# Two attention mixers of an encoder trunk: TensorE's order fixed product by product, scalings moved to ScalarE, and the per-layer input products moved into the mixers' ends

## The chip, the cores and the metric

The kernel runs on one core of one Trainium2 chip. The metric is the device time of one execution in microseconds (us), the median of several runs. The engines are named as the profile names them: PE is TensorE's matrix product, PEld its weight load, DVE is VectorE, ACT is ScalarE, POOL is GpSimd, SP is the queue that issues most transfers (DMAs).

## The reference

A trunk of two layers over 512 positions with a width of 1024, all in float32. Cut to what matters:

```python
for i in range(DEPTH):                                   # DEPTH = 2
    h = h + 0.5 * swiglu(rmsnorm(h), ffn1...)            # inner width 2816
    hn = rmsnorm(h, norm_mix[i])
    if i % 2 == 0:
        h = h + ab_mixer(hn, w_in_ab, sink_a, w_out_ab, pos)
    else:
        h = h + c_mixer(hn, w_in_c, rpb_c, w_out_c)
    h = h + 0.5 * swiglu(rmsnorm(h), ffn2...)
    gate = sigmoid(rmsnorm(h, norm_ple[i]) @ w_ple_gate[i])
    h = h + gate * (p[i] @ w_ple_proj[i])                # p[i]: 512 x 256, an input
return rmsnorm(h, norm_final)
```

`ab_mixer` projects `hn` to queries, keys and values of two kinds of attention. Kind A has 12 query heads and 4 key heads; each block of 128 queries sees its own block of keys and the neighbours, and each head has a sink logit in its softmax. Kind B has 4 slots, each with three groups of keys at strides 1, 4 and 16; the outputs of the groups are merged by weights that come from the maxima and sums of their softmaxes. `c_mixer` is attention of 16 heads over an 8 x 16 neighbourhood of a grid of width 64, with a bias from a table. Each mixer ends with a product by `w_out`. The product `p[i] @ w_ple_proj[i]` depends on inputs alone.

## The kernel before

All activations lie transposed: 8 chunks of 128 channels by 512 positions. To keep float32's accuracy each operand of a large product is split in a high part (rounded to PE's reduced float32, written by ACT) and a low part (the rest, a subtraction on DVE or POOL). One such product (`mm3`) is three matmuls: high by high, high by low, low by high (L142 to L144 of the kernel before, L322 to L324 for the values). A weight unit of 128 x 1024 (512 KB) is fetched by SP as `wr` and split into `wh` (ACT) and `wl` (DVE) at L121 and L122.

The stages in the profile, in us from the span's start: the first feed-forward part to 381, mixer ab from 381 to about 662, the second feed-forward part, the per-layer input stage (`ple`) to about 1100, then the same for layer 1 with mixer c from about 1450 to 1668 and `ple` from about 2063 to 2108, and the tail.

A mixer has two kinds of work for PE. The *fill* is the projections (24 matmuls of 512 columns each for a query or key unit, values by groups of 256 columns), which need only weights and `xg`, the scaled input. The *steps* are attention itself: for each head the scores (L428, L598), a masked maximum on DVE (L429, L602), exponentials on ACT (L568, L608), the scaling by the reciprocal of the sum on DVE (L572, 48 instructions), transposes on PE (L349) into a PSUM bank named `tr`, the split of these by ACT (L121, high) and DVE (L122, low), and the products with the values (L359, L360) into a bank named `ob`. For kind B, `merge` (L611) works out weights by small copies and products on DVE and scales the 32 blocks of exponentials on DVE (L638); `pv_r` transposes those of the strided groups (L647) and multiplies (L653).

PSUM has three banks for products (`mm`), two for scores (`sc`), two for transposes (`tr`) and one for `ob`. A bank is written again only when what it held has been read.

`weave` (L503) calls steps and fills whole, one after the other, in a proportion of weights. The instructions that come of it are put in an order on each engine by the framework's scheduler, by readiness and priority; so PE's order in the program is already mixed instruction by instruction. Once built, every engine runs its own list in order.

Of the kernel before, what the change touches and what calls it, by code (L numbers as in the profile page):

```python
# [15 lines left out]
P = 128  # L16
# [15 lines left out]
PART = .8  # L32
WARM = 12
RPB_W = 48


class Trunk:
# [3 lines left out]
    def __init__(self, ctx, tc, io):  # L41
# [6 lines left out]
        self.ap_ = pool("act", 59)  # L48
        self.tp = pool("tmp", 8)
# [10 lines left out]
        self.open = {}  # L60

# [27 lines left out]

    def setup(self):  # L90
# [5 lines left out]
        self.identb = self.cp.tile([P, P], BF16, name="identb")  # L96
        nc.vector.tensor_copy(self.identb, self.ident)
# [7 lines left out]
        idle = self.cp.tile([P, T], BF16, name="idle")  # L105
# [33 lines left out]
    def mm3(self, out, stat, mov, start, stop):  # L139

        mm = self.nc.tensor.matmul
        mm(out, stat[0], mov[0], start=start, stop=False)  # L142
        mm(out, stat[0], mov[1], start=False, stop=False)  # L143
        mm(out, stat[1], mov[0], start=False, stop=stop)  # L144
# [37 lines left out]
    def stat(self, tag, cols):  # L182
# [3 lines left out]
        for i, x in enumerate(cols):  # L186
            nc.tensor.matmul(ps[:, i:i + 1], self.acc[:, x], self.ones[:, 0:1], start=True, stop=True)
# [13 lines left out]
    def spread(self, rcol):  # L201

        n = rcol.shape[-1]
        rp = self.tbank()[:, :n * P]
        for b in range(n):
            self.nc.tensor.transpose(rp[:, b * P:(b + 1) * P], rcol[:, b:b + 1].broadcast_to([P, P]), self.ident)
        return rp
# [46 lines left out]

    def project(self, src):

        u = self.unit(src, lo_eng=self.lo_eng())
        p = self.bank()
        self.mm_unit(p, u, self.xg, True, True)
        return p  # L260

# [46 lines left out]
    def project_v(self, src, view, rcol, parts=True):  # L308
# [5 lines left out]
        for q in range(2):  # L314
            u = self.unit(src[:, q * UNIT:(q + 1) * UNIT], lo_eng=self.lo_eng())
            for kk in range(4):
                k = 4 * q + kk
                h, l = (x[:, kk * 256:(kk + 1) * 256] for x in u)
                for b in range(NB):
                    xh, xl = (view(x, b) for x in self.xg[k])  # L320
                    first, last = k == 0 and b % 2 == 0, k == KC - 1 and b % 2 == 1
                    nc.tensor.matmul(ps[b], xh, h, start=first, stop=False, skip_group_check=True)  # L322
                    nc.tensor.matmul(ps[b], xh, l, start=False, stop=False, skip_group_check=True)  # L323
                    nc.tensor.matmul(ps[b], xl, h, start=False, stop=last, skip_group_check=True)  # L324
# [18 lines left out]
    def transposed(self, blocks):  # L343
# [4 lines left out]
        for i, b in enumerate(blocks):  # L348
            nc.tensor.transpose(t[:, i * P:(i + 1) * P], b, self.ident)  # L349
        hi, lo = self.tmp(F32R), self.tmp(F32R)  # L350
# [4 lines left out]
    def pv(self, out, v, p, start, stop):  # L355


        mm = self.nc.tensor.matmul
# [3 lines left out]
    def windows_pv(self, o, es, vcol):  # L362

        for x in range(NB):
            qb = range(*self.window(x))
            blocks = []
            for b in qb:
                off = (x - self.window(b)[0]) * P
                blocks.append(es[b][:, off:off + P])
            hi, lo = self.transposed(blocks)  # L370
            self.pv(o[:, qb[0] * P:(qb[-1] + 1) * P], vcol(x), (hi, lo), x == 0, x == NB - 1)

    def out_part(self, w, m, mix, cs):
# [4 lines left out]
        for c in cs:  # L378
            ww = (u[0][:, c * P:(c + 1) * P], u[1][:, c * P:(c + 1) * P])
            self.mm3(p, ww, mix[c], c == 0, c == KC - 1)  # L380
        return p

    def out_proj(self, w, mix, done, k_next):
# [3 lines left out]
        for m in range(KC):  # L387
            p = self.out_part(w, m, mix, range(done if m < OPEN else 0, KC))
            del self.open[m]
            nc.vector.tensor_tensor(self.h[m], p, self.h[m], op=ALU.add)  # L390
            self.norm_chunk(m)

# [25 lines left out]
    def scores(self, q, k, hf, b, m):  # L418
# [6 lines left out]
        e = self.act()[:, :n]  # L425
        qq, kk = slice(b * P, (b + 1) * P), slice(lo * P, hi * P)
        for i in range(2):
            nc.tensor.matmul(s[:, :n], q[hf][:, qq], k[i][hf][:, kk], start=i == 0, stop=i == 1)  # L428
        nc.vector.tensor_tensor_reduce(e, s[:, :n], mask[:, off:off + n], op0=ALU.add, op1=ALU.max, scale=0.125,  # L429
                                       scalar=-3e38, accum_out=st)  # L430
        return e
# [5 lines left out]
    def ab(self, k_next):  # L437
# [20 lines left out]
        def proj(key, i, kind):  # L458
            return key, 1, lambda: t.__setitem__(key, self.rope(self.project(w[i]), kind))

        def proj_a(gp):
            def k_step():
                k, low = self.rope(self.project(w[12 + 4 * gp]), "n"), self.lows()
                t["ak", gp] = (self.stack_k(k, low), low)

            def q_step(j):
                t["aq", gp, j] = self.stack_q(self.rope(self.project(w[13 + 4 * gp + j]), "n"))

            return [(("ak", gp), 1, k_step)] + [(("aq", gp, j), 1, lambda j=j: q_step(j)) for j in range(3)]

        def proj_b(sp):
            def q_step():
                t["bq", sp, 0] = self.stack_q(self.rope(self.project(w[6 * sp]), "b"))

            def k_step():
                k, low = self.rope(self.project(w[6 * sp + 1]), "n"), self.lows()
                t["bk", sp, 0] = (self.stack_k(k, low), low)

            steps = [(("bk", sp, 0), 1, k_step), (("bq", sp, 0), 1, q_step)]
            for g in (1, 2):  # L480
                steps.append(proj(("bq", sp, g), 6 * sp + 2 * g, "r"))
                steps.append(proj(("bk", sp, g), 6 * sp + 2 * g + 1, "r"))
            return steps

        def proj_v(key, i):
            if i < 2:
                f = lambda: v.__setitem__(key, self.project_v(io["v_ab"][i], nat, self.rcol))
            else:
                f = lambda: v.__setitem__(key, self.residues(
                    self.project_v(io["v_ab"][i], nat, self.rcol, parts=False)))  # L490
            return [(key, 2.4, f)]

        a0, a1 = proj_a(0), proj_a(1)
        fill = (a0[:2] + proj_v("va", 0) + a0[2:] + a1 + proj_b(0) + proj_v("vb", 1) + proj_v(("vr", 0), 2)
                + proj_b(1) + proj_v(("vr", 1), 3))
        steps = (self.a_steps(0, t, v, m_a, sink, mix) + self.a_steps(1, t, v, m_a, sink, mix)
                 + self.b_steps(0, t, v, m_b0, m_br, mix) + self.b_steps(1, t, v, m_b0, m_br, mix))
        fill += [(("o", m), PART, lambda m=m: self.out_part(io["o_ab"], m, mix, range(6))) for m in range(OPEN)]
        self.weave(steps, fill, after={("o", 0): 26})
        self.out_proj(io["o_ab"], mix, 6, k_next)  # L500

    @staticmethod
    def weave(steps, fill, lead=1, after=()):  # L503


        by, after = {}, dict(after)
        for i, (needs, _, _) in enumerate(steps):
            for k in needs:
                by.setdefault(k, i)
        end = len(steps) + lead  # L510
        for i in range(len(fill) - 1, 0, -1):
            name, prev = fill[i][0], fill[i - 1][0]
            by[prev] = min(by.get(prev, end), by.get(name, end))
        total, work = sum(f[1] for f in fill), sum(s[1] for s in steps)
        n, done, past = 0, 0, 0
        for i, (_, weight, f) in enumerate(steps):
            while n < len(fill) and after.get(fill[n][0], 0) <= i and (
                    by.get(fill[n][0], end) <= i + lead or (done + fill[n][1]) * work <= past * total):
                done += fill[n][1]
                fill[n][2]()  # L520
                n += 1
            f()
            past += weight
        for _, _, f in fill[n:]:
            f()
# [6 lines left out]
    def a_steps(self, gp, t, v, m_a, sink, mix):  # L532
# [529 lines left out]
```

## Time and profile before

| what | value |
|---|---|
| median of 3 runs | 2126.14 us (2123.86 to 2126.70) |
| the profiled execution | 2126.64 us, of which the span 2124.8 us |
| mean granted clock of PE | 0.995 |
| busy PE, DVE, ACT, POOL | 98%, 53%, 37%, 17% of the span |
| mixer ab, 381 to 675 us: busy PE, DVE, ACT | 275.2, 238.1, 154.4 of 294 us |
| mixer c, 1480 to 1668 us: busy PE, DVE, ACT | 183.3, 139.3, 113.7 of 188 us |

A busy matmul is recorded from its start to a modelled end, and successive matmuls overlap. A row of a matmul of 512 columns says some 390 ns, while in a stretch without a wait one starts every 226 ns. So an idle time of PE is shorter in the record than the time that is lost. The number to compare is the stretch less the number of matmuls times their pace.

### The profile page before, as it was taken

Reading aid. Unit: us, or ns where it says so; the run is one execution under the profiler, and the core shown is the slowest. Engines: PE = TensorE matmul, PEld = TensorE weight load, DVE = VectorE, ACT = ScalarE, POOL = GpSimd, SP = SyncE. Lnnn points to the kernel's source line nnn. Section 1 sums busy time; section 2 is a strip of 40 time slices with the busy share of each in tenths; the row PEclk is TensorE's granted clock in tenths of the full one; section 3 lists DMA queues with packets and bytes.
Section 4 is the critical chain, followed back from the end, with each engine's and each line's share of the span. In section 5 each row is a group of like instructions: output and inputs, shape, how many; then the busy total and the mean of one; then the engine's idle time right before and its main releaser. Section 6 shows DMA issues by size and latency. Waiting matters only on the chain.

```text
span 2124.8 us, 25520 instructions
## 1 busy us (share of the span) xinstructions
PE 2085.4 (98%) x9950; PEld 1734.6 (82%) x9950; DVE 1132.3 (53%) x1793; ACT 783.8 (37%) x1255; POOL 352.3 (17%) x248
## 2 busy tenths in 40 slices
PE   8999999999999999999999999999999999999998
PEld 6888888777787888888888888888888888888886
DVE  6554432699786444543354555333778744553334
ACT  4332222465544333222343233223656533232232
POOL 3111101233211111101111111013222210110111
PEclk9999999999999999999999999999999999999999
DMA  5333333221223233333333322334333223323331
GB/s 171 98 99 99 95 96 98 85 75 56 65 68 92 90 99 99 99 90 96 105 97 99 99 93 93 95 97 124 105 105 102 82 90 99 99 91 96 94 107 60
DMA packets 75385, 202.02 MB, mean 95 GB/s; under 512 B 16896, under 2 KB 24576, under 8 KB 75264
## 3 DMA queue, kind: packets, MB, share of 16 engines
q1 hardware_dynamic: 74976, 200.29, 30.8%
q8 instruction: 78, 1.28, 0.3%
q14 instruction: 43, 0.35, 0.1%
q10 hardware_dynamic: 288, 0.10, 0.0%
HBM read 191.97 MB, written 2.59 MB: 92 GB/s over the span
## 4 chain that ended last, share of the span: by engine, by line
PE 89%; DVE 5%; ACT 2%; issue 1%; POOL 1%; DMA 0%; SPq 0%; DVEq 0%; POOLq 0%; ACTq 0%
PE mm L143 15%; PE mm L144 15%; PE mm L142 15%; PE sc L142 12%; PE sc L143 12%; PE sc L144 12%; PE mm L322 1%; PE mm L323 1%; PE mm L324 1%; PE tr L349 1%; PE ob L359 1%; PE ob L360 1%; PE sc L428 1%; ACT wh L121 1%; DVE act L572 1%
## 5 line engine op out<-in xcount | busy, mean ns | idle before, releaser
L121 ACT ACTIVATE wh<-wr 128x1024 fp32r<-128x1024 f32 (+1 forms) x360 | 374.6, 1042 | 995.0 <-issue 431.1
L122 DVE TENSOR_TENSOR wl<-wr,wh 128x1024 fp32r<-128x1024 f32 (+1 forms) x343 | 510.2, 1488 | 314.1 <-ACT wh L121 313.1
L143 PE MATMUL mm<-act,wh 128*128 128x512 f32 (+1 forms) x1560 | 609.7, 391 | 3.0 <-DVE act L169 2.1
L142 PE MATMUL mm<-act,wh 128*128 128x512 f32 (+1 forms) x1560 | 609.1, 391 | 1.0 <-ACT wh L121 0.6
L144 PE MATMUL mm<-act,wl 128*128 128x512 f32 (+1 forms) x1560 | 608.3, 390 | 0.5 <-DVE wl L122 0.5
L144 PE MATMUL sc<-act,wl 128*128 128x512 f32 (+1 forms) x1138 | 442.5, 389 | 0.8 <-DVE wl L122 0.8
L142 PE MATMUL sc<-act,wh 128*128 128x512 f32 (+1 forms) x1138 | 442.9, 389 | 0.0
L143 PE MATMUL sc<-act,wh 128*128 128x512 f32 (+1 forms) x1138 | 442.5, 389 | 0.0
L143 PEld LDWEIGHTS mm<-act,wh 128*128 128x128 f32 x1560 | 293.4, 188 | 64.4 <-DVE act L169 5.3
L142 PEld LDWEIGHTS mm<-act,wh 128*128 128x128 f32 x1560 | 293.3, 188 | 60.0 <-ACT act L121 1.5
L144 PEld LDWEIGHTS mm<-act,wl 128*128 128x128 f32 x1560 | 293.2, 188 | 58.4 <-DVE wl L122 1.0
L239 POOL TENSOR_TENSOR tmp<-tmp,tmp 128x512 f32<-128x512 f32 x88 | 115.2, 1309 | 818.5 <-DVE tmp L238 783.7
L144 PEld LDWEIGHTS sc<-act,wl 128*128 128x128 f32 x1138 | 213.7, 188 | 45.1 <-DVE wl L122 1.2
L143 PEld LDWEIGHTS sc<-act,wh 128*128 128x128 f32 x1138 | 213.7, 188 | 44.1
L142 PEld LDWEIGHTS sc<-act,wh 128*128 128x128 f32 x1138 | 213.6, 188 | 43.8
L238 DVE TENSOR_TENSOR tmp<-sc,R 128x512 f32<-128x512 f32 x88 | 60.8, 691 | 276.8 <-PE sc L144 276.8
L180 POOL TENSOR_TENSOR ssq<-ssq,tmp 128x512 f32<-128x512 f32 x55 | 90.2, 1639 | 552.6 <-ACT tmp L175 525.7
L236 DVE TENSOR_TENSOR tmp<-mm,R 128x512 f32<-128x512 f32 x88 | 60.8, 691 | 130.4 <-PE mm L144 127.9
L121 ACT ACTIVATE act<-tmp 128x512 fp32r<-128x512 f32 x92 | 58.3, 634 | 117.3 <-POOL tmp L239 116.2
L322 PE MATMUL mm<-wh,act 128*128 128x256 f32 x256 | 74.4, 291 | 0.3 <-DVE act L337 0.3
L323 PE MATMUL mm<-wl,act 128*128 128x256 f32 x256 | 73.9, 289 | 0.0
L324 PE MATMUL mm<-wh,act 128*128 128x256 f32 x256 | 73.8, 288 | 0.0
(142 smaller groups left out, 1621.8 us busy)
## 6 DMA issues: line engine op xcount, KB each, us to landing
wr<-in_gu_dram SPq DMA_DIRECT2D x176, 512.0 KB, 3.5
wr<-in_dn_dram SPq DMA_DIRECT2D x64, 512.0 KB, 3.5
wr<-in_dn_dram SPq DMA_DIRECT2D x32, 384.0 KB, 3.1
wr<-in_qk_ab_dram SPq DMA_DIRECT2D x20, 512.0 KB, 3.5
wr<-in_plg_dram SPq DMA_DIRECT2D x16, 512.0 KB, 3.5
wr<-in_qk_c_dram SPq DMA_DIRECT2D x16, 512.0 KB, 3.7
act<-act SPq DMA_DIRECT2D x40, 128.0 KB, 2.2
wr<-in_v_ab_dram SPq DMA_DIRECT2D x8, 512.0 KB, 3.8
```

Of the source, the lines that this page charges most:

```text
L121: self.nc.scalar.activation(hi, src, AF.Copy)
L122: (lo_eng or self.nc.vector).tensor_tensor(lo, src, hi.bitcast(F32), op=ALU.subtract)
L142: mm(out, stat[0], mov[0], start=start, stop=False)
L143: mm(out, stat[0], mov[1], start=False, stop=False)
L144: mm(out, stat[1], mov[0], start=False, stop=stop)
L180: eng.tensor_tensor(self.acc, self.acc, sq, op=ALU.add)
L236: nc.vector.tensor_tensor(t1, pgu[0], R, op=ALU.mult)
L238: nc.vector.tensor_tensor(t2, pgu[1], R, op=ALU.mult)
L239: nc.gpsimd.tensor_tensor(t2, t1, t2, op=ALU.mult)
L322: nc.tensor.matmul(ps[b], xh, h, start=first, stop=False, skip_group_check=True)
L323: nc.tensor.matmul(ps[b], xh, l, start=False, stop=False, skip_group_check=True)
L324: nc.tensor.matmul(ps[b], xl, h, start=False, stop=last, skip_group_check=True)
```

## The change

**Order.** Inside `weave` every matmul and transpose of PE is pinned to the order in which the program calls it (`pin`, `mm`, `turned`). The order is made by generators: a step or fill yields after each few instructions with the PE time in us that it takes by a table in the code (0.68 for three matmuls of 512 columns), `weave` adds that up as a clock, and lets fill go between the pieces of a step in proportion. Distances on this clock hold steps apart: `CHUNK` 10 us from a projection to the scores that need it, `SOFT` 9 from scores to their transposes, `MERGE` 22 from the last scores of kind B to the transposes of merged blocks, `SPLIT` 3.5 from transposes to the products with the values, `VR` 9. Of the steps the first that is ready among `REACH` 4 is taken. DVE, ACT, POOL and SP still have their order from the scheduler.

**Attention.** Scores, transposes and value products are separate steps. Transposes of a head are three groups of blocks, (1), (2) and (0, 3), where there were four (two of two blocks and two of three). The 48 scalings by the sum's reciprocal and the 32 scalings of `merge` move from DVE to ACT (a Copy with a scale). `merge` runs directly behind the exponentials of the second half, and `pv_r` has its four transposes ahead of the products that need them. `first_two` puts the norm's small work behind the mixer's first projection.

**The per-layer input product.** The 48 matmuls of `p[i] @ w_ple_proj[i]` per layer (`ple_proj`: 8 chunks of six) go from `ple` to the end of the mixers' fill. ACT copies each chunk to `tmp`, SP stores it to DRAM (`pp`), and `ple` loads it again (8 loads of 256 KB per layer).

**Room.** Five of the eight chunks that mixer ab hands to its output product (0, 1, 2, 3 and 6; two parts of 256 KB each) are stored to DRAM (`put_away`) and fetched before that product. The pool `act` grows from 59 to 62 tiles, `tmp` shrinks from 8 to 6. The scores of a head share three tiles (`places`), and the split transposes lie in `act` where they were in `tmp`.

The number of matmuls of each width in the mixers is the same, but for the added 96 of 512 columns that `ple` loses.

The core of the diff:

```diff
+CHUNK, SOFT, MERGE, SPLIT, VR = 10, 9, 22, 3.5, 9
+REACH = 4
...
+    def pin(self, ins):
+        if self.pinned:
+            self.tc.keep_in_program_order(ins)
+
+    def mm(self, *a, **kw):
+        self.pin(self.nc.tensor.matmul(*a, **kw))
+
+    def turned(self, out, block):
+        self.pin(self.nc.tensor.transpose(out, block, self.ident))
...
+    def mm_steps(self, out, u, xs, start, stop):
+        for i, x in enumerate(xs):
+            w = (u[0][:, i * P:(i + 1) * P], u[1][:, i * P:(i + 1) * P])
+            self.mm3(out, w, x, start and i == 0, stop and i == len(xs) - 1)
+            yield .68
...
+    GROUPS = ((1,), (2,), (0, 3))
+
+    def windows_tr(self, es):
...
+            hi, lo = self.transposed(blocks, self.act)
...
+    def ple_proj(self, i):
...
+        def chunk(m):
+            if m == 0:
+                c["p"] = []
+                for k in range(2):
+                    raw = self.tmp()
+                    nc.sync.dma_start(raw, io["pT"][i, :, k, :])
+                    c["p"].append(self.split_chunk(raw))
...
+            b = self.bank()
+            yield from self.mm_steps(b, tuple(x[:, s:s + 2 * P] for x in c["u"]), c["p"], True, True)
+            t = self.tmp()
+            nc.scalar.activation(t, b, AF.Copy)
+            nc.sync.dma_start(self.pp[i, m], t)
...
+            left.remove(s)
+            if begin is None:
+                begin = filled
+            for us in s[3]():
+                clock += us
+                past += us * s[4] / s[2]
+                while filled - begin < (total - begin) * past / work and piece():
+                    pass
+            done[s[0]] = clock
...
+        for b in range(NB):
+            nc.scalar.activation(es[b], es[b], AF.Copy, scale=rd[:, b:b + 1])
...
+            for x in range(2):
+                for hf in range(2):
+                    for i in range(4):
+                        e, ww = ((c["er", hf][i], w[:, hf, 1, i:i + 1]), (c["e0", hf][i], w0[:, hf, i:i + 1]))[x]
+                        nc.scalar.activation(e, e, AF.Copy, scale=ww)
-            for hf in range(2):
-                for i in range(4):
-                    for e, ww in ((c["er", hf][i], w[:, hf, 1, i:i + 1]), (c["e0", hf][i], w0[:, hf, i:i + 1])):
-                        nc.vector.tensor_scalar_mul(e, e, ww)
...
-                self.mm_unit(pp, upm, cut(p), True, True)
+            pm = self.tmp()
+            nc.sync.dma_start(pm, self.pp[i, m])
```

Three places show what this does to the engines' lists.

PE before, at the first transposes of a merge of kind B (L647; `act_4263` and `act_4431` hold merged exponentials, `mm_4802` is a value unit's projection as fill):

```order
L142 MATMUL mm_4802<-act_1877,wh_4797 128x512
L647 MATMUL tr_4705<-ident,act_4263 128x128 x2
L143 MATMUL mm_4802<-act_1878,wh_4797 128x512
L144 MATMUL mm_4802<-act_1877,wl_4798 128x512
L142 MATMUL mm_4802<-act_1969,wh_4797 128x512
L143 MATMUL mm_4802<-act_1970,wh_4797 128x512
```

The transposes stand inside the fill, and what of the fill is behind them waits with them. PE of the change, behind the scores of the second merge (`mm_4822` is the last value product, `mm_5162` the first chunk of the per-layer input product, `act_5146` and `act_5147` high and low part of its operand):

```order
L102 MATMUL mm_4822<-wh_5065,act_2528 128x256
L102 MATMUL mm_5162<-act_5146,wh_5157 128x512
L102 MATMUL mm_5162<-act_5147,wh_5157 128x512
L102 MATMUL mm_5162<-act_5146,wl_5158 128x512
L102 MATMUL mm_5162<-act_5152,wh_5157 128x512
```

The transposes of that merge now come 74 rows later; between the scores and this chunk stand 8 score matmuls of another head and 57 value products, so the chunk is what now fills the distance. ACT of the change at the same place (L810 is a scaling of the merge, L734 an exponential and L738 a scaling of a head of kind A, L137 a split's high part):

```order
L810 ACTIVATE act_4917<-act_4917,w_b_4989 128x256
L810 ACTIVATE act_4915<-act_4915,w_b_4989 128x384
L810 ACTIVATE act_4916<-act_4916,w_b_4989 128x384
L810 ACTIVATE act_4917<-act_4917,w_b_4989 128x256
L734 ACTIVATE act_5024,st_a_5022<-act_5024,st_a_5022 128x384
L734 ACTIVATE act_5025,st_a_5022<-act_5025,st_a_5022 128x256
L137 ACTIVATE act_5146<-tmp_5144 128x512
L738 ACTIVATE act_5025<-act_5025,st_a_5022 128x256
L738 ACTIVATE act_5023<-act_5023,st_a_5022 128x384
L738 ACTIVATE act_5024<-act_5024,st_a_5022 128x384
L738 ACTIVATE act_5025<-act_5025,st_a_5022 128x256
L137 ACTIVATE act_5152<-tmp_5150 128x512
```

The high part of the chunk's operand, `act_5146`, stands behind all 16 scalings of the merge (the last four are shown), and between the first of them and it stand also four value copies (L368) and, with the two ahead of that first one, four exponentials of the next head. Before, the scalings were on DVE and `pT` was split in `ple`. A third place, also on ACT, is the first head of kind A (`tr_2946` and `tr_2962` are the first and third group of transposes of one head; `act_2950` is the high part of the first):

```order
L137 ACTIVATE wh_3253<-wr_3252 128x1024
L305 ACTIVATE act_2930<-act_2928 64x512
L738 ACTIVATE act_2832<-act_2832,st_a_2829 128x256
L738 ACTIVATE act_2830<-act_2830,st_a_2829 128x384
L738 ACTIVATE act_2831<-act_2831,st_a_2829 128x384
L738 ACTIVATE act_2832<-act_2832,st_a_2829 128x256
L305 ACTIVATE act_2933<-act_2928 64x512
L137 ACTIVATE act_2950<-tr_2946 128x384
```

The split of a group of transposes stands behind two copies of a stacked query or key (L305) and the four scalings of the head that comes after it; on PE the third group `tr_2962` takes the bank of `tr_2946` and follows three transposes behind the second group.

More of the change, by code (lines that the diff above doesn't have):

```diff
@@ L499, in ab, with f @@
[L499 to L525, printed above, removed]
+            def f():
+                x = yield from self.project_v(io["v_ab"][i], nat, self.rcol, parts=i < 2)
+                v[key] = x if i < 2 else self.residues(x)
```

454 lines of the change are left out of this document (304 added, 150 removed).

## The prediction

> **What bounds the kernel now.** I read the page first, then the windows by stage.
>
> ```profile
> span 2124.8 us, 25520 instructions
> PE 2085.4 (98%) x9950; PEld 1734.6 (82%) x9950; DVE 1132.3 (53%) x1793; ACT 783.8 (37%) x1255; POOL 352.3 (17%) x248
> PE 89%; DVE 5%; ACT 2%; issue 1%; POOL 1%; DMA 0%; SPq 0%; DVEq 0%; POOLq 0%; ACTq 0%
> 100.00:340.00 240.00, 240.00 (x1061) 198.72 (x1060) 106.89 (x99) 69.08 (x85) 26.07 (x19) 1.00 0.32 97
> 381.00:395.00 14.00, 10.29 (x65) 8.85 (x63) 8.23 (x10) 4.06 (x6) 10.35 (x8) 0.99 0.32 94
> 395.00:500.00 105.00, 100.05 (x529) 82.85 (x530) 92.19 (x237) 63.21 (x150) 33.81 (x24) 0.98 0.21 61
> 500.00:600.00 100.00, 92.79 (x557) 79.21 (x556) 79.95 (x215) 49.85 (x124) 25.40 (x17) 0.95 0.20 61
> 600.00:675.00 75.00, 72.05 (x423) 59.88 (x422) 57.68 (x141) 37.29 (x81) 9.13 (x6) 1.00 0.24 75
> ```
>
> PE bounds the whole. The first window is feed-forward: 1061 matmuls of 512 columns in 240 us, one every 0.226 us, no idle. Only the mixers can give anything; there DVE is busy 88% of 395 to 500. A matmul costs the same wherever it stands, so what counts is each mixer's loss: the stretch less its matmuls at their pace.
>
> ```profile
> L144 PE MATMUL mm<-act,wl 128*128 128x512 f32 x184 | 73.6, 400 | 0.0
> L142 PE MATMUL sc<-act,wh 128*128 128x512 f32 x19 | 7.6, 400 | 0.0
> L322 PE MATMUL mm<-wh,act 128*128 128x256 f32 x128 | 37.9, 296 | 0.3 <-DVE act L337 0.3
> L428 PE MATMUL sc<-act,act 128*128 128x256 f32 (+1 forms) x128 | 31.2, 338 | 3.7 <-DVE act L270 2.5 <-DVE st_b L602 0.5 <-DVE st_b L429 0.5
> L349 PE MATMUL tr<-ident,act 128*128 128x128 f32 x160 | 28.3, 276 | 5.1 <-DVE act L572 5.1
> L360 PE MATMUL ob<-tmp,act 128*128 128x256 f32 (+1 forms) x64 | 21.4, 339 | 2.9 <-DVE tmp L122 2.8
> L598 PE MATMUL sc<-act,act 64*128 64x128 f32 x64 | 8.2, 278 | 0.4 <-DVE st_b L429 0.4
> L647 PE MATMUL tr<-ident,act 128*128 128x128 f32 x32 | 6.0, 296 | 4.3 <-DVE act L638 4.3
> L653 PE MATMUL ob<-tmp,act 128*64 128x128 f32 x64 | 4.9, 284 | 0.0
> 401.80 0.28 PE L322 MATMUL mm<-wh,act 128*128 128x256 f32 x1
> 403.96 0.28 PE L322 MATMUL mm<-wh,act 128*128 128x256 f32 x1
> ```
>
> These are the groups of PE by line from 381 to 675 us; L142 and L143 have 183 each beside L144's 184, all three have 19 in `sc`, L323 and L324 as many as L322, L359 as many as L360. The last two rows have 17 matmuls between them: 2.16/18 = 0.120 us for 256 columns. For the L428, L359 and L360 matmuls, half 256 and half 384 wide, I estimate 0.148; for 128 columns 0.11 (half of 0.226). 607 x 0.226 + 384 x 0.120 + 256 x 0.148 + 324 x 0.11 = 257; 294 - 257 = **37 us lost in mixer ab**. The releasers say to whom: the scalings on DVE (5.1 + 4.3), the low parts on DVE (2.8), the first low part (2.5).
>
> ```profile
> L144 PE MATMUL mm<-act,wl 128*128 128x512 f32 x152 | 59.7, 393 | 0.0
> L322 PE MATMUL mm<-wh,act 128*128 128x256 f32 x128 | 36.5, 285 | 0.0
> L798 PE MATMUL sc<-act,act 128*128 128x256 f32 x128 | 20.4, 285 | 0.1
> L349 PE MATMUL tr<-ident,act 128*128 128x128 f32 x128 | 18.4, 273 | 0.0
> L360 PE MATMUL ob<-tmp,act 128*128 128x256 f32 x64 | 16.8, 287 | 1.7 <-DVE tmp L122 1.7
> ```
>
> In mixer c (1450 to 1675; 28 more of each of the three in `sc`, 12 small ones) the same count gives 540 x 0.226 + 640 x 0.120 + 140 x 0.11 = 214 of 225: **11 us lost**. So 48 us is all that the change can win.
>
> **The change part by part.** PE's work stays what it is; the input products (48 x 0.226 = 10.9 us per layer) are moved. In `ple` they lay beside nothing that waits, so this stage only becomes shorter by as much as the mixers become longer; the 256 KB stores and loads find the DMA share (next to last column of the windows) at 0.2 to 0.3. The tail loses six matmuls that covered the last sigmoid: +0.7, half of 6 x 0.226.
>
> The price lies in who now makes PE wait. The work that goes to ACT, and the merge's chain:
>
> ```profile
> L572 DVE TENSOR_SCALAR act<-act,st_a 128x256 f32<-128x256 f32 (+1 forms) x48 | 24.1, 553 | 0.2
> L638 DVE TENSOR_SCALAR act<-act,w_b 128x256 f32<-128x256 f32 (+1 forms) x32 | 10.6, 404 | 0.1
> L121 ACT ACTIVATE tmp<-tr 128x256 fp32r<-128x256 f32 (+1 forms) x64 | 26.6, 434 | 33.1 <-PE tr L349 32.5
> L568 ACT ACTIVATE act<-act,st_a 128x256 f32<-128x256 f32 (+1 forms) x48 | 26.4, 552 | 7.0 <-DVE st_a L564 6.9
> L331 ACT ACTIVATE act<-mm,rcol 128x256 f32<-128x256 f32 x8 | 3.2, 469 | 0.0
> L649 ACT ACTIVATE tmp<-tr 128x512 f32<-128x512 f32 x8 | 4.6, 597 | 14.7 <-PE tr L647 14.6
> L122 DVE TENSOR_TENSOR tmp<-tr,tmp 128x256 fp32r<-128x256 f32 (+1 forms) x64 | 30.2, 486 | 15.8 <-ACT tmp L121 15.3
> L122 POOL TENSOR_TENSOR act<-act,act 128x512 fp32r<-128x512 f32 x6 | 8.1, 1350 | 22.7 <-ACT act L121 22.6
> L269 ACT ACTIVATE act<-act 64x512 fp32r<-64x512 f32 x16 | 10.1, 628 | 7.7 <-DVE act L409 5.1 <-DVE act L415 1.4 <-DVE st_a L564 1.0
> 558.22 0.17 DVE L605 TENSOR_SCALAR ng_b<-st_b 128x8 f32<-128x8 f32 x1
> 566.10 2.82 DVE L634 COPY w_b<-w_b 32x2 f32<-32x2 f32 x16
> 568.95 0.62 DVE L638 TENSOR_SCALAR act<-act,w_b 128x256 f32<-128x256 f32 x2
> 566.35 0.39 PE L142 MATMUL mm<-act,wh 128*128 128x512 f32 x1
> 569.36 0.69 PE L647 MATMUL tr<-ident,act 128*128 128x128 f32 x2 [2.62 <-DVE act L638]
> 570.27 0.63 PE L144 MATMUL mm<-act,wl 128*128 128x512 f32 x1
> 571.97 0.55 PE L142 MATMUL mm<-act,wh 128*128 128x512 f32 x1
> ```
>
> DVE gives up 34.7 us; ACT gets 80 scalings at an estimated 0.42 (the split's 0.434, which reads PSUM) = 34 us, on 154. By mean both fit in 294 us. What matters is ACT's own order, so each place is walked along the two lists.
>
> (1) *Start.* The norm's small work now stands under the first two units: 1.0, between 0.5 and the 2.5 of the L428 row.
>
> (2) *First half, to 457 us.* The third group of transposes takes the bank of the first, whose split stands on ACT behind two stack copies (2 x 0.63) and four scalings (4 x 0.42), and these behind the next head's exponentials; DVE's low part (0.5) comes after. If ACT comes there as PE does, it is 1.3 + 1.7 + 0.4 + 0.5 = 3.9, less the second group's three transposes, so 3 for the first head alone; if ACT still has the exponentials before it (4 x 0.55), 6, and some 1 at each of five later heads: 11. Since the later heads have fill between, I take 5.5.
>
> (3) *First merge, 457 to 500.* Behind its scores ACT has 8 exponentials, 16 scalings (6.7), two heads of kind A (16 x 0.5), value copies, splits and weight units, some 31 us for PE's 28: at least 3; 11 if each of four transpose groups finds its bank's split behind a weight unit or scalings. I take 6.
>
> (4) *500 to 560.* Transposes of strided blocks follow one another into two banks, each waiting for a copy of 0.6 us (the L649 row); scores wait for two maxima. 3 to 11; 4.5.
>
> (5) *Second merge and the first chunk.* In the rows above the weights stand at 566.10, 7.9 us after the last maximum (558.22). ACT then has 16 scalings 6.7, four value copies 4 x 0.4, four exponentials 2.2, and the split 0.5: the operand is there 19 us after the maxima. PE has only 8 scores (1.2) and 57 value matmuls (6.8) before the chunk: it waits 11. The low part (POOL, 1.35) and the second operand behind four more scalings add 2. 13 in all; 9 if the next head's exponentials and the copies are done while the chain is still on DVE, 16 with POOL late. I take 12.5. What stands behind it on PE is all of the chunks, and the transposes of both merges' halves.
>
> (6) *End.* No fill is left for the last transposes, and ten fetches of 256 KB queue on SP behind the last chunk's store: 0 (covered) to 8; 3.5.
>
> (7) *Clock.* After the 2.62 us of idle at 569.36 the next four 512-wide steps took 1.70 us (570.27 to 571.97) instead of 0.9: about 1.2 lost with the one before. Three such waits (places 2, 3, 5): 3, from 1 to 5.
>
> [...]
>
> Mixer ab then loses 1 + 5.5 + 6 + 4.5 + 12.5 + 3.5 + 3 = **36** (20 to 65). In mixer c the scalings stay on DVE; distances give the splits (L360's 1.7) their time, while the single `ob` bank and the chunk's operands add waits: **6** (3 to 10).
>
> Sum: 36 + 6 + 0.7 - 37 - 11 = -5.3, on the profiled 2126.6: 2121.3, and the median of the runs is 0.5 below it: **2121 us**.
>
> **The rivals.** (a) *The distances hold.* A merge chain of 19 us fits into 22, and everything but place 5 is covered: 20 in ab, 3 in c, 2126.1 + 23.7 - 48 = 2102. For it: DVE, named by nearly all waits, loses 15% of its work. Against it: ACT's order, read above.
>
> (b) *ACT's list becomes the bound.* At the two merges ACT has more work than PE, and every split behind scalings is late; it decides from where ACT comes to a head's split after PE has made the second transposes group. 56 in ab, 9 in c: 2126.1 + 65.7 - 48 = 2144, slower. For it: all splits, exponentials and scalings in one list in fixed order, and a pinned PE can't do other work while it waits (before, it too had a fixed order, but one chosen with the waits in view). Against: ACT is 53% busy here on average.
>
> (c) *Waits only change their releaser.* What DVE's scalings cost (9.4) ACT's cost, and the chunk's 13 takes what the distances save: 2126, same.
>
> **How the numbers follow.** Forecast 0.36, (a) 0.20, (b) 0.24, (c) 0.20. A measurement tells 0.2%, 4.2 us. The forecast stands just past that bound; of its chance I give 0.26 to faster, 0.08 to same, 0.02 to slower; of (c) 0.12 to same, 0.03 and 0.05. Faster 0.49, same 0.20, slower 0.31. The range reaches from just below (a) to (b): 2101 to 2143; the forecast's own is 2112 to 2130.
>
> **What would show it.** Right: a PE idle of about 10 us, at the first chunk of the input product, released by ACT's split (L137); idle rows of transposes released by splits and no more by scalings on DVE; DVE near 203 us and ACT near 190 in the stretch of mixer ab; feed-forward at 0.226. Wrong: no such idle (then the merge's chain or ACT's order was read wrongly, and (a) holds); idle at most transposes with ACT as releaser, (b); or waits for DMA at the output product or in `ple`, which I put near nothing.

## The result

The changed kernel takes **2228.3 us** (median of 4 runs, 2227.3 to 2229.8) where the kernel before takes 2126.4 (2123.9 to 2127.6): a ratio of 1.048 with a 95% interval of 1.046 to 1.050. It is 102 us slower. The prediction had said 2121, with a range of 2101 to 2143.

The page of the changed kernel, span, engines and chain of waits:

```profile
span 2225.5 us, 25606 instructions
PE 2116.6 (95%) x9944; PEld 1761.1 (79%) x9944; DVE 1112.1 (50%) x1694; ACT 825.1 (37%) x1335; POOL 351.2 (16%) x250
```

The span is 100.7 us longer. DVE has 20 us less to do than before (1132), ACT 41 more (784); PE's busy time grew by 31, at the same number of matmuls but for a few records (9944 and 9950). The windows by stage of the changed kernel (columns as before: busy time and count of PE, PEld, DVE, ACT, POOL, then granted clock, DMA share, GB/s):

```profile
100.00:340.00 240.00, 240.00 (x1060) 198.72 (x1060) 106.92 (x99) 69.15 (x85) 26.07 (x19) 1.00 0.32 97
395.00:500.00 105.00, 84.59 (x431) 72.52 (x431) 67.56 (x150) 57.58 (x128) 24.81 (x18) 0.90 0.20 63
500.00:600.00 100.00, 81.83 (x487) 71.64 (x485) 53.96 (x149) 52.85 (x123) 22.86 (x19) 0.90 0.21 66
600.00:675.00 75.00, 63.44 (x305) 53.92 (x305) 50.45 (x146) 32.84 (x88) 11.23 (x8) 0.82 0.17 53
675.00:755.00 80.00, 62.02 (x305) 47.36 (x306) 33.76 (x52) 45.67 (x88) 10.12 (x7) 0.94 0.36 118
1635.00:1760.00 125.00, 106.59 (x614) 91.84 (x614) 78.49 (x239) 66.56 (x153) 21.69 (x15) 0.95 0.33 99
```

Feed-forward is untouched (1060 matmuls in 240 us). In 395 to 500 us *every* engine is less busy than before in the same stretch: PE 84.6 after 100.1, DVE 67.6 after 92.2, ACT 57.6 after 63.2; in these 105 us PE gets through 431 matmuls, before 529. DVE lost more than the scalings that left it, and ACT, which got them, is no busier. No engine is the bound; they wait for each other.

Counted as in the prediction (the stretch less the matmuls at their pace), mixer ab now loses 112 us (381 to 755; 37 before) and mixer c 31 (1525 to 1760; 11 before). The remaining 6 of the 101 lie at the norms of the per-layer input stages and at the tail. What PE waited for in mixer ab (381 to 755 us; total, times, longest):

```profile
PE tr L105 <- DVE act L138: 35.2, 17, 6.0
PE sc L102 <- DVE st_a L567: 9.6, 6, 2.9
PE mm L102 <- ACT act L137: 8.3, 2, 7.8
PE sc L102 <- DVE st_b L567: 5.2, 3, 3.6
PE ob L102 <- ACT tmp L819: 4.7, 3, 2.3
```

The largest is a transpose that waits for a bank of the two `tr` banks, until DVE has taken the low part out of it. Scalings are no longer among the releasers.

### The profile page after: what moved, and what is told of

Same layout as the page of the kernel before. It is cut to its first block, busy times and chain, and to the rows that moved or that the text cites. A ratio compares the mean times of both kernels' runs of the same rounds, so it can differ in the third digit from the quotient of the medians.

```text
span 2225.5 us, 25606 instructions
## 1 busy us (share of the span) xinstructions
PE 2116.6 (95%) x9944; PEld 1761.1 (79%) x9944; DVE 1112.1 (50%) x1694; ACT 825.1 (37%) x1335; POOL 351.2 (16%) x250
## 4 chain that ended last, share of the span: by engine, by line
PE 67%; DVE 4%; issue 4%; ACT 3%; POOL 1%; DMA 1%; SPq 0%; DVEq 0%; ACTq 0%; POOLq 0%
PE mm L102 37%; PE sc L102 28%; PE ob L102 1%; PE tr L105 1%; ACT act L734 1%; ACT act L137 0%; DVE act L138 0%; ACT act L1028 0%; DVE wl L138 0%; DVE act L567 0%; ACT act L738 0%; ACT act L810 0%; DVE act L306 0%; DMA act<-act 0%; ACT wh L137 0%
## 5 line engine op out<-in xcount | busy, mean ns | idle before, releaser
L102 PE MATMUL mm<-act,wh 128*128 128x512 f32 x3040 | 960.5, 397 | 20.6 <-ACT act L137 11.2
L137 ACT ACTIVATE wh<-wr 128x1024 fp32r<-128x1024 f32 (+1 forms) x360 | 374.3, 1041 | 979.3 <-issue 440.7
L102 PE MATMUL sc<-act,wh 128*128 128x512 f32 (+1 forms) x2352 | 722.5, 388 | 0.0
L102 PE MATMUL mm<-act,wl 128*128 128x512 f32 x1520 | 598.6, 394 | 0.5 <-DVE wl L138 0.5
L102 PE MATMUL sc<-act,wl 128*128 128x512 f32 x1176 | 456.1, 388 | 0.0
L102 PE MATMUL mm<-wh,act 128*128 128x256 f32 x512 | 103.2, 291 | 1.4 <-DVE act L374 1.4
L137 ACT ACTIVATE act<-tmp 128x512 fp32r<-128x512 f32 x92 | 58.1, 633 | 116.4 <-POOL tmp L255 116.4
L102 PEld LDWEIGHTS mm<-wh,act 128*128 128x128 f32 x512 | 85.7, 198 | 2.1 <-issue 1.7
L105 PE MATMUL tr<-ident,act 128*128 128x128 f32 x320 | 49.9, 288 | 38.0 <-DVE act L138 38.0
L102 PE MATMUL sc<-act,act 128*128 128x256 f32 (+2 forms) x320 | 67.4, 341 | 19.6 <-DVE st_a L567 9.6
L102 PEld LDWEIGHTS sc<-act,act 128*128 128x128 f32 (+1 forms) x320 | 54.2, 222 | 30.4 <-DVE st_a L567 12.3
L105 PEld LDWEIGHTS tr<-ident,act 128*128 128x128 f32 x320 | 37.8, 146 | 48.4 <-DVE act L138 43.3
```

The lines of the kernel that those rows point to most:

```text
L102: self.pin(self.nc.tensor.matmul(*a, **kw))
L105: self.pin(self.nc.tensor.transpose(out, block, self.ident))
L137: self.nc.scalar.activation(hi, src, AF.Copy)
```

## The experiments

The theory that the runs were to test first, P: pinning makes every late piece of work on ACT or DVE PE's wait, since the fill behind the waiting instruction can't go first. The rivals: S, that the 80 scalings on ACT delay the splits, and I, that the moved input products are the cause.

### Without the pin, and the other two parts alone

```diff
     def pin(self, ins):
-        if self.pinned:
-            self.tc.keep_in_program_order(ins)
+        pass
```

> The changed kernel with the pinning of PE's order taken out and all else kept: steps, distances, scalings on ACT, input products in the mixers. Theory P (the pinned order is the cause: a late split stops all of PE, since the fill behind it can't go first): most of the 102 us come back, 2120 to 2150 us, and the 35 us in which transposes wait for the split's low part on DVE fall under 10. Theory S (the scalings on ACT make every split late): not much changes, 2200 or more. Theory I (the input products in the mixers): 2200 or more.

```diff
-            nc.scalar.activation(es[b], es[b], AF.Copy, scale=rd[:, b:b + 1])
+            nc.vector.tensor_scalar_mul(es[b], es[b], rd[:, b:b + 1])
...
-                        nc.scalar.activation(e, e, AF.Copy, scale=ww)
+                        nc.vector.tensor_scalar_mul(e, e, ww)
```

> The changed kernel, pinned, with all 80 scalings back on DVE. Theory S: 2160 us or less, since the splits' high parts on ACT are no longer behind scalings. Theory P: 2200 to 2250, the wait changes its releaser (transposes wait for scalings on DVE) but not its size.

```diff
-        fill += self.ple_proj(1)
...
-                pm = self.tmp()
-                nc.sync.dma_start(pm, self.pp[i, m])
+                self.mm_unit(pp, upm, cut(p), True, True)
```

> The changed kernel, pinned, with the input products back in the per-layer input stage (no stores, no loads of chunks). Theory I: 2180 us or less. Theories P and S: the waits at the chunks go (8 + 2 in mixer ab, 6 in mixer c) and about 4 at the norms of the input stages, but the fill that the products were at the mixers' ends is gone too: 2205 to 2235.

| run | time, us | against the changed kernel |
|---|---|---|
| without the pin | 2157.0 (2151.9 to 2159.1; 1.014 of before, 1.013 to 1.016) | -71 |
| pinned, scalings on DVE | 2240.8 (one run) | +13 |
| pinned, input products back | 2219.4 (one run) | -9 |

The pin alone is 71 of the 102 us. That is most of them, as theory P has it, but the time lies 7 us above P's range. S falls: with the scalings on DVE the pinned kernel was slower in the one run made. I is worth 9 us at most, far from the 2180 or less that it asked for. The first head of kind A shows the mechanism. PE and ACT of the changed kernel (start, duration):

```profile
416.18 0.82 PE L105 MATMUL tr<-ident,act 128*128 128x128 f32 x6
423.00 1.11 PE L105 MATMUL tr<-ident,act 128*128 128x128 f32 x4 [6.00 <-DVE act L138]
416.55 1.05 ACT L137 ACTIVATE wh<-wr 128x1024 fp32r<-128x1024 f32 x1
418.56 0.63 ACT L305 ACTIVATE act<-act 64x512 fp32r<-64x512 f32 x1 [0.97 <-DVE act L543]
419.09 1.90 ACT L738 ACTIVATE act<-act,st_a 128x256 f32<-128x256 f32 x4
421.01 0.63 ACT L305 ACTIVATE act<-act 64x512 fp32r<-64x512 f32 x1
421.66 0.87 ACT L137 ACTIVATE act<-tr 128x384 fp32r<-128x384 f32 x2
```

and PE without the pin, with ACT's split of the first group in the last row but two:

```profile
414.85 0.82 PE L104 MATMUL tr<-ident,act 128*128 128x128 f32 x6
415.43 0.83 PE L101 MATMUL sc<-act,act 128*128 128x256 f32 x4
416.10 0.63 PE L101 MATMUL mm<-act,wh 128*128 128x512 f32 x2
420.90 0.44 PE L101 MATMUL ob<-act,act 128*128 128x384 f32 x1 [0.52 <-ACT act L136]
421.88 0.60 PE L104 MATMUL tr<-ident,act 128*128 128x128 f32 x4
420.36 0.87 ACT L136 ACTIVATE act<-tr 128x384 fp32r<-128x384 f32 x2
PE tr L104 <- DVE act L137: 4.4, 8, 1.2
PE mm L101 <- ACT act L136: 16.0, 3, 11.6
```

Pinned, the third group follows the first two at once, and PE stands for 6.0 us, while ACT works off a weight unit, two copies and the next head's four scalings ahead of the split. Without the pin the scheduler puts the next scores and 18 fill matmuls and more in front of that group. The split comes no sooner, 5.5 us after the first transposes in both kernels (416.18 to 421.66, 414.85 to 420.36), but PE has work meanwhile. The last two rows are sums over the whole unpinned kernel: transposes wait 4.4 us for low parts, in place of 35.2 in mixer ab alone.

Counted step by step from 381 us to the tail, the steps of PE with a wait of over 0.3 us before them lost 103 us against their pace in the changed kernel and 57 without the pin (26 before). The steps that began while the granted clock was at half, with no such wait, lost 38 and 9 (6 before). So of the 71 us some 46 are waits, and nearly 30 the half clock that came with them.

Whether a wait also makes the next one is seen less directly, on the engines that feed PE. The maxima on DVE before, then the maxima and the exponentials on ACT in the changed kernel, then without the pin (window of mixer ab; the last numbers are the engine's own idle time and for what; ACT's row of before, L568 with 7.0, is in the prediction):

```profile
L429 DVE CUSTOM_DVE_ANT_0 act<-sc,act 128x256 f32<-128x256 f32 (+1 forms) x64 | 29.6, 483 | 5.6 <-PE sc L428 5.1
```

```profile
L567 DVE CUSTOM_DVE_ANT_0 act<-sc,act 128x256 f32<-128x256 f32 (+1 forms) x64 | 30.3, 488 | 23.5 <-PE sc L102 23.0
L734 ACT ACTIVATE act<-act,st_a 128x256 f32<-128x256 f32 (+1 forms) x48 | 26.4, 553 | 19.4 <-DVE st_a L730 19.4
```

```profile
L566 DVE CUSTOM_DVE_ANT_0 act<-sc,act 128x256 f32<-128x256 f32 (+1 forms) x64 | 29.9, 485 | 6.9 <-PE sc L101 6.5
L733 ACT ACTIVATE act<-act,st_a 128x256 f32<-128x256 f32 (+1 forms) x48 | 26.4, 554 | 7.0 <-DVE st_a L729 7.0
```

The maxima on DVE wait 23.5 us for PE's scores in the pinned kernel, 5.6 before and 6.9 without the pin; the exponentials wait 19.4 us for the step behind the maxima, 7.0 in both others. While PE stands at a transpose, the scores behind it aren't made; so DVE has no maxima to take, ACT no exponentials, and the next split may be late again. The instructions' own durations are the same. This loop fits the rows but isn't shown by them alone: the same work in a longer stretch leaves DVE more idle in any case (160 of 374 us pinned, 105 of 309 without the pin, 56 of 294 before).

### What is left without the pin

Without the pin 31 us remain over the kernel before. Its largest wait was 11.6 us (the row of `mm` among the sums above) at the first chunk of the input product, for the operand's split on ACT. Two runs took on that remainder: one with the operand split early,

```diff
+        def parts():
+            c["p"] = []
+            for k in range(2):
+                raw = self.tmp()
+                nc.sync.dma_start(raw, io["pT"][i, :, k, :])
+                c["p"].append(self.split_chunk(raw))
+            yield 0.
...
-                q(1, 0), proj_v("vb", 1), proj_v(("vr", 0), 2), ...
+                q(1, 0), proj_v("vb", 1), *pt, proj_v(("vr", 0), 2), ...
```

> The changed kernel without pinning, and with the loads and splits of the input product's operand taken out of the first chunk: they are a fill of their own, ahead of the value units (in mixer ab before the value unit of the first merge, in mixer c before the last two heads). If the 11.7 us at the first chunk is what place 5 of the prediction says (the operand's split stands on ACT behind the second merge), then 11 to 15 us go in mixer ab and 4 to 7 in mixer c: 2135 to 2143 against 2157. If PE would wait there for something else anyway (the transposes, the values), under 6 us come back: 2150 or more.

and one without the pin and with the input products back in their stage (the two edits shown above together).

> The changed kernel without pinning and with the input products back in their stage: what is left is the finer weave with its distances, separate steps, scalings on ACT, the start and the store and fetch of five chunks. If the 31 us that are left over the kernel before lie with the input products (13 in ab, 8 to 10 in c, 6 at norms and tail): 2125 to 2135. If they lie with the weave, its distances or the fetches: 2145 or more.

The early split gives 2142.1 us (two runs, 1.008 of before, 1.005 to 1.011): 15 of the 31 back, as place 5 of the prediction asked. But PE again stands at the same spot, at the fourth chunk:

```profile
622.66 6.92 ACT L812 ACTIVATE act<-act,w_b 128x256 f32<-128x256 f32 x16
630.57 0.57 ACT L458 ACTIVATE tmp<-mm 128x512 f32<-128x512 f32 x1
631.19 0.79 PE L101 MATMUL mm<-act,wh 128*128 128x512 f32 x1 [7.40 <-ACT tmp L458]
```

The first row is ACT with the merge's 16 scalings in one go, the second the first copy of a chunk out of its bank, behind them; of three `mm` banks none is free for the fourth chunk. With the input products out altogether it is 2144.6 (two runs; 1.009, 1.006 to 1.012), between the two expectations, at the edge of the second, and the wait has another name once more:

```profile
PE mm L100 <- DMA act<-away: 12.3, 1, 12.3
```

Without those chunks the output product is the next fill, and its fetched operands aren't there yet. So in three forms PE lacks 7 to 12 us of work that is ready between the second merge's scores and its transposes, whatever was put there. Would it help to take the scalings of the merge off ACT there?

```diff
-                        nc.scalar.activation(e, e, AF.Copy, scale=ww)
+                        nc.vector.tensor_scalar_mul(e, e, ww)
```

> The run without pinning and with the early split (2142 us, in which PE waits 7.4 us for ACT's copy of a chunk of the input product behind the second merge), with the 32 scalings of the merges back on DVE. If ACT's list at the merge is the wait: the 7.4 us fall under 3 and the time to 2132 to 2138. If PE is only too early for the merge whoever scales: 2140 to 2146.

2140.5 us (two runs), as the second reading had it: the wait for the copy falls from 7.4 to 1.1, but 1.5 us is all that comes of it, hardly more than the runs differ among themselves. Score matmuls wait 10.4 us for the maxima on DVE (7.0 with the scalings on ACT), and others are spread. So it doesn't matter here who scales; that PE's lead over the merge is the limit is argued from this, and no run changed that lead.

### Pinned, with the distances changed

If the pinned order only had its distances too short, longer ones would help. The groups of a head's transposes apart (at "hold" `weave` calls fill for 3.4 us of its clock), and then also the transposes farther from the scores:

```diff
             yield .11 * len(blocks)
+            if g == (2,):
+                yield ("hold", 3.4)
```

> The changed kernel, pinned, but with 3.4 us of fill called between the second and the third group of a head's transposes in mixer ab, so that the first group's bank has time to be read. If PE's waits at the third group are only a matter of distance between the groups, the 35 us of transposes behind the split's low part fall to under 15 and the time to 2195 to 2210. If the split is late because ACT and DVE hold other work before it, whatever stands between, the wait moves to the next pinned instruction and the time stays over 2215.

```diff
-CHUNK, SOFT, MERGE, SPLIT, VR = 10, 9, 22, 3.5, 9
+CHUNK, SOFT, MERGE, SPLIT, VR = 10, 14, 22, 3.5, 9
```

> The changed kernel, pinned, with 3.4 us of fill between the groups (2215 us) and the distance from scores to transposes raised from 9 to 14 us. If the distances are simply short for the real chains: 2185 to 2200. If what is late is decided by the lists on ACT and DVE, which the scheduler builds anew for every order of PE, the waits only move: 2205 to 2230.

The spaced groups: 2215.2 us; spaced with 14: 2221.6 (one run each). PE's waits over the whole execution of the first (the three that bear on this):

```profile
PE sc L102 <- DVE st_a L574: 16.0, 9, 4.3
PE sc L102 <- DVE st_b L574: 9.4, 5, 4.6
PE tr L105 <- DVE act L138: 8.4, 10, 2.6
```

Spacing did what it was to do, the transposes' wait fell to 8.4 us, but only 13 us of time came back, and scores now wait 25 us for maxima (15 in mixer ab of the changed kernel): the first reading's waits, the second reading's time. With 14 us the time went up by 6, as the second reading of that run had it, and the transposes' wait is back at 17.9. The early split in the pinned kernel tells the same:

> The changed kernel, pinned, with the input product's operand split early as in the run without pinning. The waits at the first chunks (8 + 2 in mixer ab, 3 + 3 in mixer c) go: 2210 to 2218 against 2228. If PE then stands at the next pinned transposes instead, 2222 or more.

2226.4 us (one run), 2 less, which is within the spread of the changed kernel's runs, where the same edit without the pin gave 15. The waits moved on, as its second reading had it: transposes wait 38.6 us for low parts over the whole execution, 38.0 in the changed kernel.

### The kernel before, pinned, and with single parts of the change

Pinning PE in both weaves of the kernel before, where steps are called whole:

> The kernel before with PE pinned to its program's order in both mixers' weaves, where steps and fills are called whole. If a pinned order makes every late split PE's wait: each of the 48 + 32 groups of transposes is followed at once by the products that need it, and costs 1.5 to 2 us (high part 0.5, low part 0.6, and the way there), 120 to 160 us, and the scores and merges some 50 more: 2280 to 2350. If PE's order in the kernel before hardly differs from the program's: under 2200.

2407.0 us (one run), 280 over the kernel before, and 57 above the upper expectation. Its two largest waits:

```profile
PE ob L45 <- ACT tmp L145: 64.4, 86, 1.6
PE ob L45 <- DVE tmp L146: 26.6, 28, 2.1
```

The single waits are shorter than the 1.5 to 2 us expected. Counted as above, its waits lose 186 us (26 before) and the half clock 131 (6 before; the granted clock is 0.70, 0.72 and 0.67 in 395 to 500, 500 to 600 and 600 to 675 us). The changed kernel, pinned too, is 180 us faster than this. Most of that is likely its product-by-product weave, since the scalings and the input products moved its time by only 13 and 9 us; it just doesn't reach what the scheduler's own order gives.

Two parts of the change were put in the kernel before alone: the 80 scalings on ACT (the reverse of the edit above),

> The kernel before with all 80 scalings on ACT and nothing else changed. The prediction's reading (DVE bounds the first half of mixer ab, and 9.4 us of idle are released by scalings on DVE): 2110 to 2124 us. If ACT's single list is as tight as DVE's: 2124 to 2135. Theory S: 2150 or more even without pinning.

and with them the order at the start of mixer ab (`first_two`: the norm's small work after the first projection, and the spread of it in the middle of the second).

> The kernel before with all 80 scalings on ACT (2122.8 us alone) and, of mixer ab of the change, the order at its start: the norm's small work behind the first projection and in the middle of the second. Mixer ab of the change lost 1.0 us between 375 and 400 where the kernel before loses 5.9, so if that gain stands by itself: 2116 to 2120 us. If the work only waits later (the first scores need the same rotated query): 2121 to 2125.

The scalings on ACT: 2122.8 us, 0.9986 of before (0.9976 to 0.9995; 10 runs against 13). This is the only kernel here whose interval lies below the kernel before, by some 3 us, within the range that the prediction's reading of DVE gave. Where the 3 us come from isn't shown: the ten runs reach from 2120.1 to 2127.5, and the profile is of one with 2127.4. With the start as well: 2126.4, 0.9995 (0.9985 to 1.0004; 11 runs), which tells no difference from before and lies above both expectations; in its profile the stretch 375 to 400 loses some 4.4 us where it lost 5.9 before and 1.0 in the change, so little of the start's gain stands by itself, and the time doesn't show it.

## Why the prediction was wrong

*What bounds the kernel, and the loss of 37 + 11 us:* right as a count of what could be won. The step from there, "so 48 us is all that the change can win", had no counterpart for what it could lose, and the sum took the waits of the new order as a short list.

*Place by place.* The losses of the changed kernel, between the same places in PE's list (the rows end at some 406, 500, 560, 640, 707 and 755 us), in us. The last two columns say what of it lies in steps with a wait of over 0.3 us before them, and in steps at half clock without one:

| place | predicted (low to high) | measured | waits | half clock |
|---|---|---|---|---|
| (1) start | 1.0 (0.5 to 2.5) | 4.6 | 3 | 1 |
| (2) first half | 5.5 (3 to 11) | 26.8 | 20 | 6 |
| (3) first merge | 6 (3 to 11) | 19.7 | 12 | 6 |
| (4) between the merges | 4.5 (3 to 11) | 26.2 | 18 | 8 |
| (5) second merge, first chunk | 12.5 (9 to 16) | 27.5 | 17 | 10 |
| (6) end | 3.5 (0 to 8) | 7.3 | 6 | 0 |
| (7) clock | 3 (1 to 5) | in the rows above | | 32 in sum |
| mixer c | 6 (3 to 10) | 31 | 22 | 6 |

*The first wait of a chain was sized well, the ones after it were not.* The upper bound for the first head in (2) was 6: it took 6.0 (the lower one, 3, is 3.6 by the prediction's own terms). That is partly luck: the exponentials which the bound counted had ended (416.6), and a weight unit of 1.05 and ACT's own wait of 0.97 for DVE stood in their place. For the first chunk in (5) the prediction had the operand 19 us after the last maximum and a wait of 11; the rows are these:

```profile
665.13 0.17 DVE L774 TENSOR_SCALAR ng_b<-st_b 128x8 f32<-128x8 f32 x1
675.81 5.31 ACT L810 ACTIVATE act<-act,w_b 128x256 f32<-128x256 f32 x12
682.10 0.63 ACT L137 ACTIVATE act<-tmp 128x512 fp32r<-128x512 f32 x1
682.78 0.79 PE L102 MATMUL mm<-act,wh 128*128 128x512 f32 x1 [7.83 <-ACT act L137]
```

17.6 us after the maximum, a wait of 7.8 pinned and 11.6 without the pin. The step that failed is in (2), "Since the later heads have fill between, I take 5.5", and its like in (3) and (4). The fill is there, but it is at most three matmuls between one group of transposes and the next. The fifth head:

```profile
474.87 0.49 PE L105 MATMUL tr<-ident,act 128*128 128x128 f32 x3
475.11 0.71 PE L102 MATMUL mm<-act,wh 128*128 128x512 f32 x2
475.66 0.39 PE L102 MATMUL mm<-act,wl 128*128 128x512 f32 x1
480.52 0.66 PE L105 MATMUL tr<-ident,act 128*128 128x128 f32 x4 [3.44 <-DVE act L138]
```

The second group, with three more matmuls, stands between the last two rows. So PE comes to the third group at most 2 us after the first, while the first group's low part is there only after 2.8 to 5.5 us at the later heads up to 500 us; ACT had here again a weight unit, a copy and the next head's four scalings ahead of the split. Up to there transposes waited five more times, 12 us in all (18.2 with the first), where the upper bound of (2) had 1 at each. The second step that failed is (7), "Three such waits": half clock followed shorter waits as well, those of 1.83 and 2.03 us at 402.32 and 491.43 among them.

All four signs that the prediction named for being right came about: the idle at the first chunk behind ACT's split (7.8 us), transposes waiting for splits and not for scalings, DVE and ACT busy for 214 and 193 us in mixer ab, and feed-forward at its pace. The time was 107 us off all the same. The signs tell which waits there are, and not what they add up to.

*The mechanism of rival (b)* had the right sign and said one true thing, that a pinned PE can't do other work while it waits. It blamed ACT's list at the merges, priced 2144, and as a cause this was wrong: ACT's list does hold the splits back, as the rows show, but with the scalings back on DVE the pinned kernel took 13 us more, and its transposes still waited 40.3 us for low parts. Its remark that PE had a fixed order before as well, "but one chosen with the waits in view", is what decides, and it was left without a price. The rows with which to price it were at hand: PE's list of the change has three groups of transposes into two banks, with nothing or at most three matmuls between one and the next in the whole of the first half. A reader can see there that PE stops at the third group for nearly the whole of a split, whatever the split waits for.

Rivals (a) and (c) fell with the sign: the distances don't hold, and the waits grew in sum, not only in name.

*The clock* was mis-sized by the most: 3 us for three waits, and 38 measured in the two mixers. No run shows the 5 us of its upper end; the prediction's own row gives some 1.2 for one wait. The window of mixer ab (381 to 755 us):

```profile
381.00:755.00 374.00, 305.12 (x1595) 256.54 (x1594) 214.01 (x502) 193.29 (x432) 79.36 (x58) 0.90 0.23 75
```

The granted clock is 0.90 over these 374 us, and was 0.98 over the 294 before; mixer c has 0.97 after 1.00. Steps at half clock without a wait lost 38 us after and 6 before, so the clock is some 30 of the 102 us, and "a matmul costs the same wherever it stands" didn't hold. It came with the waits, and short ones were enough: behind an idle of 1.83 us, at 402.32, the matmuls of 256 columns took 0.21 us each for about 3 us, in place of 0.12. After the 7.83 us of idle, PE's steps were these:

```profile
687.57 1.05 PE L102 MATMUL mm<-act,wh 128*128 128x512 f32 x2
688.43 0.63 PE L102 MATMUL mm<-act,wl 128*128 128x512 f32 x1
688.85 0.87 PE L102 MATMUL mm<-act,wh 128*128 128x512 f32 x2
689.56 0.40 PE L102 MATMUL mm<-act,wl 128*128 128x512 f32 x1
689.80 0.63 PE L102 MATMUL mm<-act,wh 128*128 128x512 f32 x2
```

At 687.57 still 0.43 us for each, from 689.56 on 0.23: half pace for 6.5 us from the end of the idle, through two waits of 0.55 that lie in it.

*What was moved at no cost* wasn't quite that: at the norm of each per-layer input stage PE now stands idle for 1.7 us for the reciprocal root (POOL), where the kernel before has no such idle, and the tail lost some 2.5 where 0.7 was foreseen.

What stays open is why the kernel without the pin, with its early split, is still 16 us over the kernel before. About 6 lie at the norms and the tail and 7 at the second merge, as shown; the finer weave's distances were not tried one by one without the pin, nor was the store and fetch of the five chunks taken out. Nor does a run separate a wait that makes the next one from a wait that would have come anyway.

## What to carry to other kernels

The fixed order for the bounding engine cost 46 us in waits here, and nearly two thirds as much again in the half clock that came with them; price such an order by the list (how much work stands between an instruction that can be late and the one that it waits for?), not by the distances meant for it. A wait that is seen on one engine's row need not be worth its length: of the 35 us of transposes, spacing them gave 13, and of the 8 + 2 at the first chunk an early split gave 2 in the pinned kernel and 15 in the free one. When all engines' busy shares fall together, look for how they wait for one another before looking for a bound.

## What the runs showed of the hardware

A tiny instruction on DVE took as long as a large one on POOL beside it. In the changed kernel (start, duration):

```profile
448.97 1.26 POOL L138 TENSOR_TENSOR act<-act,act 128x512 fp32r<-128x512 f32 x1 [4.39 <-ACT act L137]
448.98 1.27 DVE L735 TENSOR_TENSOR st_a<-st_a 128x4 f32<-128x4 f32 x1
450.28 0.18 DVE L736 RECIPROCAL st_a<-st_a 128x4 f32<-128x4 f32 x1
450.38 0.53 DVE L138 TENSOR_TENSOR act<-tr,act 128x384 fp32r<-128x384 f32 x1
```

The sum of a 128 x 4 tile starts with a POOL subtraction and ends with it, 1.27 us; the nine of the 12 that had no POOL work beside them took 0.14 to 0.16, the two others 0.89 (416.93, beside a POOL instruction that ends at 417.79) and 0.73 (474.96, beside one that ends at 475.67). The low part that PE was waiting for stands right behind. Why the two end together isn't shown by a run. The prediction's walk of the first half has no term for this step.
